# Two transformer blocks on one core: compression products in units of four, zero-padded keys, six held down-projection units, new order offsets

## The chip, the cores and the metric

The kernel runs on one core of a Trainium2 chip. The time is device microseconds (us) of one execution; the number that counts is the median of several runs. Weights and activations lie in HBM at the start and the result is written back to HBM.

## What is computed

The reference applies two layers of a first block and then two layers of a second block to one sequence of 256 tokens of width 1024, all in float32. The part that matters here, cut down:

```python
# first block, per layer (i = 0, 1)
z = rms_norm(h) @ w_in                      # 1024 -> 2328: q, k, v, gates, two MLP halves
kc = compress(zkc, ...); vc = compress(zvc, ...)
def compress(t, pe, w1, b1, w2, b2):        # 15 blocks of 32 tokens per group, 2 groups
    flat = (blocks + pe).reshape(..., 32 * 64)
    return gelu(flat @ w1 + b1) @ w2 + b2   # w1: 2048 x 256
s_s = q @ k_sel.T ; s_w = q @ k_win.T       # 8 heads of 64, 2 key groups, causal mask
attn = gated sum of softmax(s) @ v over the compressed, selected and window keys
h = h + rms_norm(concat(attn, spatial_gating(zu, zv)) @ w_o)
h = h + rms_norm((silu(g) * up) @ w_down)   # g, up: causal convolution over h @ w_up, 1024 -> 2 x 2816
h = h + sigmoid(rms_norm(h) @ w_ple_gate) * (p @ w_ple_proj)
# second block, per layer: another mixer (MLA attention, gated linear attention, pooling),
# then an FFN of the same width without convolution
```

## The kernel before

Every operation is written down by a recorder (class `Recorder`) and put into an order by a list scheduler (`schedule`, line 370), which gives each operation a start from estimated durations, and takes, on each engine, the ready operation of the lowest priority number. The priority is the operation's place in the recording plus an offset from the table `SHIFT`, keyed by phase, group and kind; `HOLD` delays operations and `ALT` moves single operations to another engine (a cast from ScalarE to VectorE, a subtraction from VectorE to GpSimd). The phases are `m1` (first block's mixer), `f1`, `f1m`, `f1e` (its FFN), `p1` (its last gate, called the gate below), `m2` and `f2`... (second block). `emit` (line 523) then issues everything in that order; so all instructions have line 529 in the profile, and are told apart by the tiles they write and read. An operation recorded as `tensor.multi` is several products that stay together.

A weight of 512 KB is loaded into one of 7 buffers `raw`, split into a rounded high part `wh` and a remainder `wl` (5 buffers each; ScalarE casts, VectorE or GpSimd subtracts), and a linear layer is the sum of three products, high by high, high by low and low by high. These products are of type float32r. Others (transposes, attention, compression) are plain float32, which TensorE runs as two passes; the trace shows each pass as a row of its own. PSUM has four pairs of banks: `pa`, `pb`, `upp`, `trp`.

`first_mix` (line 1297) weaves generators: the q projection with `compress_g(0)`, then `qk_g` and `attend_g(0)` with another projection and `compress_g(1)`, then `attend_g(1)` with the rest (lines 1578 to 1583). In `compress_g` (line 1349) four weights of 512 KB are loaded for each of the two inputs (keys, values). Each has four products with 32 stationary columns, which write four strips of 32 partitions of one bank `trp`; the loop records each product separately, so the scheduler may put others between them. There are 2 layers x 2 inputs x 16 = 64 of them. In `attend_g` the scores of a head are one product: queries of 64 partitions (the head's key group `gp`) by both kinds of keys, 256 columns for the first block of queries and 512 for the second, followed by a bf16 product that adds the mask. There are 2 layers x 2 x 8 = 32 score products.

`ffn` (line 1180) goes over 22 units of 128 hidden features: up products into `upp` and `trp`, then the unit's down products into `pa` (first 128 tokens) and `pb` (second). The down products of the last `HELD` units are kept back: first all of the first 128 tokens, then the others, so that the norm after the first half runs beside the products of the second. What follows (the gate, or the next layer's first linear) needs that norm. The held units' weights are split into spare buffers for `HELD - 2` units and into `wh`, `wl` for the last two.

Of the kernel before, what the change touches and what calls it, by code (L numbers as in the profile page):

```python
# [10 lines left out]
F32R = mybir.dt.float32r  # L11
# [13 lines left out]
HELD = 4  # L25
# [497 lines left out]
def emit(nc, order):  # L523
    for op in order:
# [10 lines left out]
        (0, 0): -76, (0, 2): -1938  # L535
    },
# [4 lines left out]
    },  # L541
# [4 lines left out]
    },  # L546
    "f1m": {
        (1, 0): 3412, (1, 2): -723, (2, 0): -26, (2, 1): 256, (2, 2): -722
    },
# [10 lines left out]
    },  # L560
# [4 lines left out]
    },  # L565
    "f2m": {
        (1, 0): -378, (1, 1): -788, (1, 2): 5203, (2, 0): -2486, (2, 1): -3052
    },
# [261 lines left out]
def tile_two_blocks(ctx: ExitStack, tc: tile.TileContext, A: dict, C: dict, out: bass.AP, stop=None):  # L830
    rec = Recorder()
# [1222 lines left out]
```

## Time and profile before

| what | value |
|---|---|
| runs | 1598.17 us median of 3 (1595.35 to 1600.52) |
| profiled execution, its own time | 1594.12 us |
| its span, first to last instruction | 1592.3 us |
[...]
| TensorE (PE) busy | 1563.9 us, 98% |
| VectorE (DVE), ScalarE (ACT), GpSimd (POOL) busy | 75%, 47%, 27% |
| DMA queues, share of 16 engines | 54% |

A row of the timeline gives the start, the length from the first start to the last end, and how many equal instructions were merged. Products overlap in the pipeline: a product's length is longer than the time until the next one starts, so what it costs is the distance between starts.

### The profile page before, as it was taken

What the parts mean: (1) busy time and instruction counts of PE and PEld (TensorE: products, weight loads), DVE (VectorE), ACT (ScalarE), POOL (GpSimd) and SP (SyncE); (2) the same over time, 40 slices, a digit from 0 to 9 for tenths busy, and PEclk for the clock granted to TensorE, in tenths of its full rate; (3) what the DMA queues carried; (4) which work ended last, traced back from release to release, by engine and by line L of the source; (5) the groups of instructions that cost most, each with busy time, mean ns of one, the idle gap of its engine ahead of it and who ended that gap; (6) DMA issues with size and microseconds to landing.
All of it is one profiled execution on the core that took longest, in us unless ns stands there. A gap on an engine that the chain in (4) does not pass through costs nothing.

```text
span 1592.3 us, 22128 instructions
## 1 busy us (share of the span) xinstructions
PE 1563.9 (98%) x8093; PEld 1273.6 (80%) x8093; DVE 1200.0 (75%) x1881; ACT 746.2 (47%) x1391; POOL 428.8 (27%) x379
## 2 busy tenths in 40 slices
PE   7999999999999999999999999999999999999998
PEld 5667888878667888878887888888888788888886
DVE  5668988898668988898576667778876666577786
ACT  4445665655445665655444234433354343353432
POOL 2222011113232011113243223233432332332423
PEclk9999999999999999999999999999999999999999
DMA  6654666645553666645544455656645444556561
GB/s 228 199 170 126 186 188 186 216 142 153 183 165 105 188 185 188 209 148 163 166 147 146 133 185 178 204 174 185 202 153 178 131 151 148 180 178 191 185 190 62
DMA packets 264149, 270.44 MB, mean 170 GB/s; under 512 B 11767, under 2 KB 196713, under 8 KB 264041
## 3 DMA queue, kind: packets, MB, share of 16 engines
q1 hardware_dynamic: 264041, 269.04, 54.3%
q8 instruction: 63, 1.03, 0.3%
q14 instruction: 45, 0.37, 0.1%
HBM read 267.95 MB, written 1.05 MB: 169 GB/s over the span
## 4 chain that ended last, share of the span: by engine, by line
PE 90%; DVE 4%; ACT 2%; POOL 1%; issue 1%; DMA 1%; SPq 0%; DVEq 0%; POOLq 0%; ACTq 0%
PE pa L529 35%; PE upp L529 20%; PE trp L529 18%; PE pb L529 17%; DVE u L529 1%; DVE wl L529 1%; POOL u L529 1%; ACT junk L529 1%; ACT wh L529 1%; ACT u L529 0%; DVE c_h L529 0%; POOL sm L529 0%; ACT x L529 0%; DMA raw<-in_w_in_dram 0%; DMA c_pi<-in_positions_dram 0%
## 5 line engine op out<-in xcount | busy, mean ns | idle before, releaser
L529 DVE TENSOR_TENSOR wl<-raw,wh 128x1024 fp32r<-128x1024 f32 (+2 forms) x408 | 510.1, 1258 | 108.0 <-ACT wh L529 106.3
L529 ACT CAST wh<-raw 128x1024 fp32r<-128x1024 f32 (+2 forms) x342 | 348.8, 1025 | 354.2 <-PE pb L529 107.1
L529 PE MATMUL pa<-wh,x 128*128 128x512 f32 (+1 forms) x1280 | 434.1, 405 | 5.2 <-ACT wh L529 3.3
L529 PEld LDWEIGHTS pa<-wh,x 128*128 128x128 f32 x1280 | 237.1, 189 | 62.9 <-issue 10.9
L529 POOL TENSOR_TENSOR wl<-raw,wh 128x1024 fp32r<-128x1024 f32 (+3 forms) x72 | 174.7, 2428 | 317.7 <-ACT wh L529 171.7
L529 PE MATMUL pa<-wl,x 128*128 128x512 f32 (+1 forms) x640 | 249.2, 402 | 0.0
L529 PE MATMUL upp<-x,wh 128*128 128x512 f32 x640 | 231.7, 397 | 0.0
L529 PE MATMUL trp<-x,wh 128*128 128x512 f32 x640 | 231.0, 397 | 0.0
L529 POOL TENSOR_TENSOR u<-u,u 128x256 f32<-128x256 f32 (+2 forms) x72 | 86.8, 1206 | 411.0 <-DVE u L529 258.0
L529 PE MATMUL upp<-x,wl 128*128 128x256 f32 x640 | 179.7, 281 | 0.0
L529 PE MATMUL trp<-x,wl 128*128 128x256 f32 x640 | 179.3, 280 | 0.0
L529 DVE CAST wh<-raw 128x1024 fp32r<-128x1024 f32 (+1 forms) x138 | 112.9, 819 | 75.8 <-PE pa L529 37.3
L529 PE MATMUL pb<-wh,x 128*128 128x512 f32 (+2 forms) x496 | 161.9, 382 | 2.8 <-ACT x L529 2.8
L529 PEld LDWEIGHTS upp<-x,wh 128*128 128x128 f32 x640 | 120.1, 188 | 26.9
L529 PEld LDWEIGHTS trp<-x,wh 128*128 128x128 f32 x640 | 119.9, 188 | 26.8
L529 PEld LDWEIGHTS pa<-wl,x 128*128 128x128 f32 x640 | 120.4, 189 | 25.8 <-issue 4.3
L529 PEld LDWEIGHTS upp<-x,wl 128*128 128x128 f32 x640 | 120.7, 189 | 4.8 <-DVE wl L529 0.6
L529 PEld LDWEIGHTS trp<-x,wl 128*128 128x128 f32 x640 | 120.8, 189 | 3.4
L529 PEld LDWEIGHTS pb<-wh,x 128*128 128x128 f32 x496 | 92.5, 189 | 19.5 <-ACT x L529 3.3
L529 DVE TENSOR_TENSOR u<-u,u 128x512 f32<-128x512 f32 (+4 forms) x160 | 101.8, 641 | 5.0 <-ACT u L529 3.7
L529 PE MATMUL pb<-wl,x 128*128 128x512 f32 (+2 forms) x248 | 91.7, 380 | 0.0
L529 ACT ACTIVATE u<-pa,sm 128x512 f32<-128x512 f32 (+2 forms) x62 | 41.2, 674 | 87.9 <-PE pa L529 87.1
(221 smaller groups left out, 2384.9 us busy)
## 6 DMA issues: line engine op xcount, KB each, us to landing
raw<-in_w_in_dram SPq DMA_DIRECT2D x112, 512.0 KB, 3.6
raw<-in_w_up_dram SPq DMA_DIRECT2D x88, 512.0 KB, 4.0
raw<-in_w_ffn_gu_dram SPq DMA_DIRECT2D x88, 512.0 KB, 4.3
raw<-in_w_down_dram SPq DMA_DIRECT2D x44, 512.0 KB, 3.5
raw<-in_w_ffn_down_dram SPq DMA_DIRECT2D x44, 512.0 KB, 4.1
raw<-in_w_o_dram SPq DMA_DIRECT2D x32, 512.0 KB, 3.5
raw<-in_cmp_w_dram SPq DMA_DIRECT2D x16, 512.0 KB, 5.1
raw<-in_w_ple_gate_dram SPq DMA_DIRECT2D x16, 512.0 KB, 3.6
```

What stands on the lines that cost most here:

```text
L529: f(*args, **kw)
```

## The change

Four things, and a new order.

In `compress_g` the four products of a loaded weight become one `multi`, so that no other TensorE operation stands between them. In `qk_g` the transposed keys go to two tiles instead of one, one for each key group, with the other group's 64 partitions set to zero (two GpSimd memsets and two VectorE copies of half the partitions in place of one copy, per half of the tokens); the score product then runs over all 128 partitions of the queries, the padded ones adding nothing. `HELD` goes from 4 to 6: the down products of six units are kept back, the last four units' weights are loaded but split only after the loop, and buffers `ah` and `al` go from 5 to 7. Each held unit gets a group of its own in the recording, so that offsets can apply to it. The planner's duration for the second block's attention products is 145 instead of 112 ns for one. The tables `SHIFT`, `HOLD` and `ALT` are all new.

```diff
-HELD = 4
+HELD = 6
...
-    AH = cls("ah", 5, 256, F32R)
-    AL = cls("al", 5, 256, F32R)
+    AH = cls("ah", 7, 256, F32R)
+    AL = cls("al", 7, 256, F32R)
...
-                hv, lv = split(load(wd[:, ft:ft + 1, :]), spare=ft in fts[-HELD:2 - HELD])
-                pend.append((ft, ah, al, hv, lv))
+                raw = load(wd[:, ft:ft + 1, :])
+                if ft in fts[2 - HELD:]:
+                    pend.append((ft, ah, al, raw))
+                else:
+                    pend.append((ft, ah, al) + split(raw, spare=ft in fts[-HELD:2 - HELD]))
...
+        for n, a in enumerate(pend):
+            rec.group += 1
+            if len(a) == 4:
+                pend[n] = a[:3] + split(a[3])
         for t in range(T):
+            for a in pend:
+                rec.group += 1
+                down_mm(*a, ts=[t])
             rec.group += 1
-            for a in pend:
-                down_mm(*a, ts=[t])
...
-        qT, kT = [], unit("kT").rearrange("p (b n) -> p b n", b=2)
+        qT, kT = [], [unit("kT").rearrange("p (b n) -> p b n", b=2) for g in range(2)]
...
-                nc.vector.tensor_copy(kT[:, :, tok(t)], ps[:, 0:2])
+                for g in range(2):
+                    gp, go = slice(g * 64, (g + 1) * 64), slice((1 - g) * 64, (2 - g) * 64)
+                    nc.gpsimd.memset(kT[g][go, :, tok(t)], 0.0)
+                    nc.vector.tensor_copy(kT[g][gp, :, tok(t)], ps[gp, 0:2])
...
-                for r in range(4):
-                    nc.tensor.matmul(ps1[32 * r:32 * r + 32, :256], X[:, 4 * mq + r], raw[:, r], start=(mq == 0),
-                                     stop=(mq == 3))
+                nc.tensor.multi([mm(ps1[32 * r:32 * r + 32, :256], X[:, 4 * mq + r], raw[:, r], start=(mq == 0),
+                                    stop=(mq == 3)) for r in range(4)], 436.0)
...
-                    nc.tensor.matmul(S[:, e], qT[t][gp, j0 + e], kT[gp, :, 0:(t + 1) * 128], start=True, stop=False)
+                    nc.tensor.matmul(S[:, e], qT[t][:, j0 + e], kT[g][:, :, 0:(t + 1) * 128], start=True, stop=False)
...
-                nc.tensor.multi(calls, 2 * 112.0 * len(calls) / 2)
+                nc.tensor.multi(calls, 145.0 * len(calls))
...
 SHIFT = {
     "c1": {
-        (0, 0): -76, (0, 2): -1938
+        (0, 0): 150, (0, 2): -97
     },
```

What the new order does at three places:

TensorE, compression of the first layer's keys (`raw` is a compression weight, `u` the blocks, 32 columns of output partitions each; `upp` belongs to a projection). Before:

```order
L529 MATMUL upp1_223<-wh3_68,x81_76 128x280
L529 MATMUL trp0_224<-raw0_58,u3_82 32x256
L529 MATMUL upp0_222<-wl2_72,x80_75 128x280
L529 MATMUL upp1_223<-wh2_67,x80_75 128x280
L529 MATMUL trp0_224<-raw0_58,u3_82 32x256
L529 MATMUL upp0_222<-wh2_67,x80_75 128x280
L529 MATMUL upp1_223<-wl2_72,x80_75 128x280
L529 MATMUL trp0_224<-raw0_58,u3_82 32x256
L529 MATMUL trp0_224<-raw2_60,u3_82 32x256 x4
L529 MATMUL upp0_222<-wh2_67,x80_75 128x280
L529 MATMUL upp1_223<-wh2_67,x80_75 128x280
L529 MATMUL trp0_224<-raw4_62,u3_82 32x256
```

With the change:

```order
L529 MATMUL upp1_227<-wh3_68,x80_75 128x280
L529 MATMUL trp0_228<-raw0_58,u5_84 32x256 x4
L529 MATMUL trp0_228<-raw1_59,u5_84 32x256 x4
L529 MATMUL upp0_226<-wl2_72,x80_75 128x280
L529 MATMUL trp0_228<-raw5_63,u5_84 32x256 x4
L529 MATMUL trp0_228<-raw6_64,u5_84 32x256 x4
L529 MATMUL upp0_226<-wh3_68,x80_75 128x280
```

Sixteen products that stood singly or in fours and fives among projection products now stand in two runs of eight with one product between them; the other three compressions have two runs of eight each too, so there are 8 such runs in the program.

TensorE, the end of the first FFN (`ah`, `al` by `wh`, `wl` into `pb` are held down products of the second 128 tokens, `c_h` is the residual whose transposes begin the gate, `x` by `wh` the gate's first products). Before:

```order
L529 MATMUL pb0_220<-wl0_70,ah2_108 128x512
L529 MATMUL pb1_221<-wl0_70,ah2_108 128x512
L529 MATMUL pb0_220<-wh0_65,al2_113 128x512
L529 MATMUL pb1_221<-wh0_65,al2_113 128x512
L529 MATMUL trp1_225<-c_ident0_185,c_h0_186 128x128 x4
L529 MATMUL trp0_224<-c_ident0_185,c_h0_186 128x128 x4
L529 MATMUL pb1_221<-wh0_65,x80_75 128x512
L529 MATMUL pa0_218<-wh3_68,x80_75 128x512
L529 MATMUL pa0_218<-wl3_73,x80_75 128x512
L529 MATMUL pa0_218<-wh3_68,x80_75 128x512 x2
L529 MATMUL pa0_218<-wl3_73,x80_75 128x512
```

With the change:

```order
L529 MATMUL pb0_224<-wh3_68,al6_119 128x512
L529 MATMUL pb1_225<-wh3_68,al6_119 128x512
L529 MATMUL pb0_224<-wh0_65,ah1_107 128x512
L529 MATMUL trp0_228<-c_ident0_189,c_h0_190 128x128 x4
L529 MATMUL pb0_224<-wl3_73,ah1_107 128x512
L529 MATMUL pb0_224<-wh0_65,al1_114 128x512
L529 MATMUL pb1_225<-wh0_65,ah1_107 128x512
L529 MATMUL pb1_225<-wl3_73,ah1_107 128x512
L529 MATMUL pb1_225<-wh0_65,al1_114 128x512
L529 MATMUL trp1_229<-c_ident0_189,c_h0_190 128x128 x4
L529 MATMUL pa1_223<-wh2_67,x80_75 128x512
L529 MATMUL pa1_223<-wl0_70,x80_75 128x512
```

Five held products now stand between the transposes of the first and of the second group of features, where the eight transposes stood together.

ScalarE, the start of the program (`raw` is the first weight, `junk` the sums of squares of the input `c_h`, `x` the normalised input). Before:

```order
L529 ACTIVATE junk0_184,sm0_118<-c_h0_186 128x512
L529 COPY c_cols_pre_mix_g0_189<-trp0_224 128x16
L529 ACTIVATE junk0_184,sm0_118<-c_h0_186 128x512
L529 ACTIVATE junk0_184,sm2_120<-c_h0_186 128x512
L529 CAST x80_75<-u4_83 128x4x128
L529 ACTIVATE junk0_184,sm2_120<-c_h0_186 128x512
L529 CAST x80_75<-u6_85 128x4x128
L529 CAST x81_76<-u7_86 128x4x128
L529 CAST wh1_66<-raw1_59 128x1024
L529 CAST wh0_65<-raw0_58 128x1024
```

With the change:

```order
L529 CAST wh0_65<-raw0_58 128x1024
L529 CAST c_ident_b0_195<-c_ident0_189 128x128
L529 ACTIVATE junk0_188,sm0_122<-c_h0_190 128x512
L529 COPY c_cols_pre_mix_g0_193<-trp0_228 128x16
L529 ACTIVATE junk0_188,sm0_122<-c_h0_190 128x512
L529 ACTIVATE junk0_188,sm2_124<-c_h0_190 128x512
L529 CAST x80_75<-u6_85 128x4x128
L529 ACTIVATE junk0_188,sm2_124<-c_h0_190 128x512
L529 CAST x81_76<-u7_86 128x4x128
L529 CAST wh2_67<-raw2_60 128x1024
```

The first weight's cast now stands ahead of everything; its load is the first in SyncE's queue too, ahead of the identity, the gains and the four loads of the input, where it was behind them.

## Rows read from the trace of the kernel before

**Rows 1.** The page's busy times, and the shares of the chain that ended last.
```profile
PE 1563.9 (98%) x8093; PEld 1273.6 (80%) x8093; DVE 1200.0 (75%) x1881; ACT 746.2 (47%) x1391; POOL 428.8 (27%) x379
...
PE 90%; DVE 4%; ACT 2%; POOL 1%; issue 1%; DMA 1%; SPq 0%; DVEq 0%; POOLq 0%; ACTq 0%
```

**Rows 2.** Two stretches: length; busy PE, PEld, DVE, ACT, POOL; clock; DMA share; GB/s.
```profile
40.00:60.00 20.00, 20.00 (x106) 13.31 (x107) 10.73 (x22) 5.42 (x10) 2.37 (x5) 1.00 0.91 293
60.00:80.00 20.00, 20.00 (x80) 10.87 (x78) 16.30 (x32) 11.22 (x45) 6.14 (x9) 1.00 0.32 100
```

**Rows 3.** A wait of PE: us in total, times, longest.
```profile
PE pb L529 <- ACT x L529: 2.8, 2, 1.4
```

**Rows 4.** Timeline of PE, compression products one by one: start, length, operation.
```profile
90.06 0.49 PE L529 MATMUL pa<-wh,x 128*128 128x512 f32 x1
90.49 0.62 PE L529 MATMUL trp<-raw,u 128*32 128x256 f32 x2
91.03 0.49 PE L529 MATMUL pa<-wl,x 128*128 128x512 f32 x1
```

**Rows 5.** Timeline of PE, five compression products (ten passes) in a run.
```profile
43.00 0.28 PE L529 MATMUL upp<-wl,x 128*128 128x280 f32 x1
43.22 1.05 PE L529 MATMUL trp<-raw,u 128*32 128x256 f32 x10
44.20 0.52 PE L529 MATMUL upp<-wh,x 128*128 128x280 f32 x2
44.65 0.62 PE L529 MATMUL trp<-raw,u 128*32 128x256 f32 x2
```

**Rows 6.** Timeline of PE, score products over 64 partitions, 256 columns.
```profile
62.51 0.28 PE L529 MATMUL upp<-c_causal_b,c_ident_b 128*128 128x256 bf16 x1
62.72 0.70 PE L529 MATMUL upp<-u,u 64*128 64x256 f32 x2
63.35 0.28 PE L529 MATMUL upp<-c_causal_b,c_ident_b 128*128 128x256 bf16 x1
```

**Rows 7.** Timeline of PE: a 64-partition product of 512 columns, then one over 128 partitions.
```profile
115.78 1.12 PE L529 MATMUL upp<-u,u 64*128 64x512 f32 x2
116.84 0.28 PE L529 MATMUL upp<-c_causal_b,c_ident_b 128*128 128x256 bf16 x1
116.96 1.02 PE L529 MATMUL pa<-u,u 128*128 128x512 f32 x2
117.82 0.38 PE L529 MATMUL trp<-c_ident,u 128*128 128x128 f32 x2
```

**Rows 8.** Timeline of PE, a float32 product of 256 columns over 128 partitions.
```profile
852.11 0.60 PE L529 MATMUL upp<-u,c_gla_tri 128*128 128x256 f32 x2
852.54 0.59 PE L529 MATMUL upp<-u,c_gla_a 128*128 128x256 f32 x2
```

**Rows 9.** Groups by form: ScalarE's casts, VectorE's subtracts, GpSimd's memsets; busy us, mean ns.
```profile
L529 ACT CAST wh<-raw 128x1024 fp32r<-128x1024 f32 x316 | 330.6, 1051 | 334.2 <-PE pb L529 102.2 <-PE pa L529 82.3 <-PE trp L529 54.9
...
L529 DVE TENSOR_TENSOR wl<-raw,wh 128x1024 fp32r<-128x1024 f32 x384 | 490.9, 1285 | 105.5 <-ACT wh L529 104.0
...
L529 POOL MEMSET u<- 64x256 f32 x14 | 6.2, 447 | 0.5
```

**Rows 10.** Timeline of PE, the end of the first FFN and the start of its gate.
```profile
346.59 0.39 PE L529 MATMUL pa<-wh,al 128*128 128x512 f32 x1
346.82 0.40 PE L529 MATMUL pa<-wh,ah 128*128 128x512 f32 x1
...
352.96 0.50 PE L529 MATMUL pb<-wh,x 128*128 128x512 f32 x1 [1.44 <-ACT x L529]
```

**Rows 11.** Timeline of PE, the first linear product of the program.
```profile
14.22 1.22 PE L529 MATMUL pa<-wh,x 128*128 128x512 f32 x2 [3.33 <-ACT wh L529]
```

**Rows 12.** DMA issues, KB each and median us to landing; the first stretch's DMA share, GB/s.
```profile
raw<-in_cmp_w_dram SPq DMA_DIRECT2D x16, 512.0 KB, 5.1
...
0.00:14.00 14.00, 4.40 (x17) 3.17 (x17) 5.72 (x14) 7.82 (x15) 3.53 (x10) 1.00 0.79 276
```

More of the change, by code (lines that the diff above doesn't have):

```diff
@@ L534 @@
     "c1": {
-        (0, 0): -76, (0, 2): -1938
+        (0, 0): 150, (0, 2): -97
     },
     "f1": {
[3 rows of a table removed]
[3 rows of a table added]
     },
     "f1e": {
[3 rows of a table removed]
[6 rows of a table added]
     },
     "f1m": {
-        (1, 0): 3412, (1, 2): -723, (2, 0): -26, (2, 1): 256, (2, 2): -722
+        (1, 0): 1282, (1, 1): -68, (1, 2): -723, (2, 1): 135, (2, 2): -728
     },
     "f2": {
[9 rows of a table removed]
[9 rows of a table added]
     },
     "f2e": {
[3 rows of a table removed]
-    },
-    "f2m": {
-        (1, 0): -378, (1, 1): -788, (1, 2): 5203, (2, 0): -2486, (2, 1): -3052
[6 rows of a table added]
     },
     "m1": {
[21 rows of a table removed]
[21 rows of a table added]
     },
     "m2": {
[38 rows of a table removed]
[38 rows of a table added]
     },
     "p1": {
[5 rows of a table removed]
[5 rows of a table added]
     },
     "s": {
-        (0, 0): -2115, (0, 2): -1198
+        (0, 0): -391, (0, 2): 1037
     },
     "s2": {
-        (0, 0): -141
+        (0, 0): -161, (0, 2): -2255
     },
@@ L646 @@
 HOLD = {
-    "c1": {
-        (0, 2): 138
-    },
     "f1": {
-        (0, 0): 94, (1, 2): 845, (2, 2): 374, (8, 2): 173, (13, 1): 186
+        (1, 2): 909, (2, 2): 66, (3, 1): 1497, (4, 2): 1406, (6, 2): 818, (12, 2): 171, (14, 0): 824, (14, 1):
+        1184
     },
     "f1e": {
-        (1, 0): 134, (2, 1): 75, (3, 1): 1197, (5, 0): 596, (5, 1): 589, (11, 2): 30, (12, 2): 33, (13, 2): 32
+        (2, 1): 741, (6, 0): 206, (6, 1): 750, (8, 1): 365, (12, 1): 204, (13, 1): 106, (16, 2): 328, (17, 2):
+        36, (19, 2): 566, (22, 2): 335, (23, 2): 102, (25, 2): 394, (28, 2): 37, (29, 2): 260
     },
     "f1m": {
-        (1, 0): 1493, (1, 1): 240, (2, 0): 110, (2, 1): 445
+        (1, 1): 240, (2, 1): 437
     },
     "f2": {
[4 rows of a table removed]
[4 rows of a table added]
     },
     "f2e": {
-        (1, 1): 325, (2, 1): 2288, (4, 1): 1742, (6, 0): 256, (9, 2): 588, (11, 2): 634, (12, 2): 259
-    },
-    "f2m": {
-        (1, 0): 91, (2, 0): 137, (2, 1): 1887
+        (2, 0): 1664, (4, 1): 280, (5, 1): 226, (14, 1): 36, (26, 2): 30, (33, 2): 702, (34, 2): 26
     },
     "m1": {
[7 rows of a table removed]
[7 rows of a table added]
     },
     "m2": {
[14 rows of a table removed]
[15 rows of a table added]
     },
     "p1": {
-        (3, 2): 2, (6, 2): 126, (7, 0): 591, (7, 1): 281, (8, 0): 60, (10, 1): 1394, (12, 1): 384, (13, 0): 909,
-        (20, 2): 169
+        (6, 2): 832, (9, 0): 162, (10, 0): 673, (10, 2): 210, (12, 0): 76, (14, 0): 10, (15, 0): 90, (15, 1):
+        76, (18, 2): 153, (20, 2): 431
     },
     "s": {
-        (0, 2): 600
+        (0, 2): 439
     },
     "s2": {
-        (0, 0): 254, (0, 2): 458
+        (0, 2): 458
     },
@@ L708 @@
     "c1": {
-        7
+        7, 13
     },
     "f1": {
-        3, 25, 28, 61, 75, 79, 82, 121, 140, 196
+        3, 11, 25, 61, 100, 121, 125, 136, 140, 196
     },
     "f1e": {
-        50, 51, 87, 120, 155, 186, 244, 255, 300, 310, 311, 356, 367, 400
+        1, 19, 40, 70, 87, 118, 137, 155, 186, 254, 261, 310, 311
     },
     "f1m": {
-        51, 110, 118
+        51
     },
     "f2": {
-        13, 32, 35, 130, 131, 170, 191, 212, 216, 241, 262, 279, 307, 325, 347, 364, 372, 431, 432, 455, 457,
-        458, 472, 513, 515, 516, 534, 555, 578, 581, 605, 637, 662, 664, 667, 702, 720, 724, 726, 728, 744, 764,
-        765, 786, 787, 823
[3 rows of a table added]
     },
     "f2e": {
-        19, 22, 40, 45, 48, 84, 106, 108, 126, 143, 164, 169, 170, 173, 187, 226, 231, 232, 234, 259, 280, 281,
-        284, 288, 305, 308, 331, 335
-    },
-    "f2m": {
-        2, 22, 40, 45, 48, 63, 81, 85, 106, 108, 110
+        22, 48, 63, 85, 102, 106, 164, 168, 169, 170, 187, 188, 209, 226, 230, 231, 232, 255, 258, 281, 282,
+        286, 303, 329, 372, 376, 377, 378, 381, 402, 420, 425, 433, 476
     },
     "m1": {
[4 rows of a table removed]
[4 rows of a table added]
     },
     "m2": {
[7 rows of a table removed]
[7 rows of a table added]
     },
     "p1": {
-        16, 18, 32, 37, 100, 103, 105, 123, 142
+        16, 18, 37, 39, 100, 142, 169
     },
     "s": {
-        6, 11, 12, 27
+        5, 27
     },
     "s2": {
-        18, 21, 34, 35, 36, 43, 48
+        7, 18, 21, 27, 33, 34, 35, 36, 48
     },
```

246 rows, old and new, of tables (ALT, HOLD, SHIFT) are left out of this document.

## The prediction

> **What bounds the kernel now.** Of the page I read the busy times and the chain first: PE is busy for 1563.9 of the 1592.3 us of the span, and 90% of the chain that ended last is PE [rows 1]. So PE bounds it, and only 1592.3 − 1563.9 = 28.4 us are idle in PE. The granted clock is 1.00 in the stretches that I use [rows 2]; nothing is to be had there. The waits of PE come next: the longest after the start are two of 1.4 us for ScalarE's `x` [rows 3], one at each end of a first-block FFN. Then comes the timeline of PE, start to start, because with a full pipeline a product costs what it holds back the next one; the busy sums hide that. What the reader is to see: a change can gain by shortening what TensorE issues, and by some microseconds at the borders. A few hundred products of the mixers are odd (32 columns, 64 partitions), and these are what the change touches.
>
> **A, compression in runs.** Each of the 64 products has 32 stationary columns and two passes. Alone among full products: from one `pa` product to the next, with a compression product between, 91.03 − 90.06 = 0.97 us [rows 4]; a full 512-column product costs 346.82 − 346.59 = 0.23 [rows 10], so 0.97 − 0.23 = 0.74 is the single's price. In a run of five: from 43.00 to 44.65 lie ten passes and three `upp` products of 280 columns [rows 5]; these are estimated at 0.23 × 280/512 = 0.13 each, so 1.65 − 0.39 = 1.26, say 1.2, for five: the passes of different strips start together. By the issue order of the kernel before, one layer has 15 singles, two runs of five, a four and a three. At 0.74, 1.2, and 0.75 for a four and for a three (a single's length, as no strip gets more than one) this is 11.1 + 2.4 + 1.5 = 15.0, and 30.0 for two layers. After, there are 8 runs of eight in the program. In a run of eight each strip gets two products, as the fullest strip in a run of five does: 1.2 each, 9.6 in all. **30.0 − 9.6 = 20.4 us less.** Bounds: if the second four begins only when the first ends, a run costs 2 × 0.75 = 1.5 and the gain is 18; if eight cost no more than four (0.75 each), it is 24. I take 20.4, as the five is the nearest row.
>
> **B, padded keys.** The 32 score products change from 64 partitions to 128, with equal columns: 16 of 256 and 16 of 512. Over 64 partitions 256 columns take 63.35 − 62.72 = 0.63 [rows 6] and 512 columns 116.84 − 115.78 = 1.06 [rows 7]; over 128 partitions the same widths take 852.54 − 852.11 = 0.43 [rows 8] and 117.82 − 116.96 = 0.86 [rows 7]. Each is 0.20 dearer over 64. The mask product ahead of a 64-partition one costs 62.72 − 62.51 = 0.21 [rows 6], ahead of a full one 116.96 − 116.84 = 0.12 [rows 7]; so entering costs 0.09 more. (0.20 + 0.09) × 32 = **9.3 us less**. Bounds: 6.4 if the entry cost comes from something else; 11 if leaving adds 0.05 that I don't separate.
> The row shows that no two 64-partition products run beside each other here: they start 0.63 and 1.06 apart, more than full ones. [...]
> Padding adds 8 memsets of GpSimd (two keys' groups, two token halves, two layers) at 0.45 us [rows 9], 3.6 us on an engine that is 27% busy [rows 1], and replaces 4 copies of VectorE by 8 of half the partitions; VectorE has 9.3 and 3.7 us of 20 free in the two stretches [rows 2]. I put both at nothing. If the cover is gone, the price is a memset and a copy ahead of the scores, under 1 us in each of 4 places: 4 us.
>
> **C, six held units, borders.** At the end of the first FFN the gate's first product waits 1.44 us for ScalarE's `x` [rows 10], and the second layer's the like: 2.8 us in two waits [rows 3]. Now five held products, 5 × 0.23 = 1.15 us, stand between the two groups of transposes; that work is only moved, so it covers up to 1.15 of each wait: **2 us less**. Bounds: 2.8 if both waits go; the other way, four of the held units are split only after the loop. If the splits come late, PE waits for a cast of 1.05 and a subtract of 1.29 [rows 9]: 2.3 us at each of the four FFNs, 9 us more. I stay near the gain, because other held units' products stand ahead of the late splits as cover: a unit has six products for one token half, 6 × 0.23 = 1.4 us, and the next split is made beside them.
>
> **D, start.** The first linear product starts at 14.22 us, after 3.33 of waiting for ScalarE's cast `wh` [rows 11]. That cast now leads ScalarE's order, and its load SyncE's queue: at best 3.3 less. But the 512 KB stand ahead of the identity, the gains and the input, and this stretch moves 276 GB/s [rows 12]: 512 KB / 276 = 1.9 us later for them, 1.9 more at worst. I take **1 less**; the norm of the input, which needs that input, then ends last.
>
> **The rest.** The other 7,500 or so TensorE products are the same in number and shape; 145 for 112 ns in the planner's book and all the tables only change the order. Zero, by some 3 us either way, since PE's small waits there are a few us altogether.
>
> Sum: −20.4 − 9.3 − 2 − 1 = −32.7. The profiled execution took 1594.1 us; the median 1598.2 stands 4.1 above it. So 1561.4 for a profile, and **1565.5** for the median. Ends of the sum: all gains at their best, 24 + 11 + 2.8 + 3.3 + 3 = 44 less, 1554; all at their worst, 18 + 6.4 − 4 − 9 − 1.9 − 3 = 6.5 less, 1592; they will not all fall together, and the forecast's own range is 1556 to 1574.
>
> **The rivals.**
> 1. *Half the gain.* Once PE needs some 15 us less per mixer of the first block, another engine or the loads end last there. For it: in 40 to 60 us DMA is at 0.91, in 60 to 80 VectorE is busy for 16.3 of 20 us [rows 2]; such stretches can shrink by 9% and 18% only. Against: they are two of many, and the neighbours have room. Then only A stays: 1598.2 − 20.4 = 1578.
> 2. *Slower: the buffers.* A run of eight needs two compression weights in `raw` at once, and the order keeps up to four of the seven buffers with them; such a load takes 5.1 us to land [rows 12]. The projections' weights behind them start late and PE waits ahead of each of the 8 runs. It decides when a run loses over 32.7 / 8 = 4.1 us; at a whole landing, 5.1, it gives 1565.5 + 41 = 1606. For it the DMA share of 0.91; against it that no wait of PE for a load stands among those now, and that the singles also held a buffer until the last of four.
> 3. *A full-array product costs double the 64-partition one.* Then B turns from −9.3 to 16 × (0.63 + 1.06) = +27, and the time is 1565.5 + 9.3 + 27 = 1602. [...]
> 4. *The strips don't overlap in runs* (the change doesn't do what it says): A is nothing, 1565.5 + 20.4 = 1586. The five in 1.2 us speaks against it [rows 5].
> 5. *More.* The order also closes most of the waits at start and borders and small ones elsewhere: of 28.4 idle us some 10 more go, 1555.
>
> **How the numbers follow.** Chances: forecast 0.74, rival 1 0.13, 2 0.03, 3 0.02, 4 0.03, 5 0.05. A measurement of this kernel tells some 0.3%, 4.8 us, from no change. Faster takes the forecast and rivals 1, 4 and 5: 0.95; rival 3, 4 us up, is same: 0.02; rival 2 slower: 0.03. The range leaves out rivals 2 to 4 and the far ends of the rest: 1554 to 1581.
>
> **What would show it.** Right: PE busy falls by some 30 us with PE still above 97%; each run of eight spans about 1.2 us start to start; padded score products stand 0.43 and 0.86 apart; the waits for `x` at the FFN ends are under 0.5; the first linear product stands near 13. Wrong: PE waits for `raw` ahead of the compression, DMA at 0.95 through the mixer (rivals 1, 2), padded products at 1.2 and over (3), runs of eight over 4 us (4), or waits on `wl` at the FFN ends (C's bound).

## The result and the profile after

The changed kernel takes **1550.52 us** (median of 4 runs, 1549.35 to 1551.15) against 1597.12 (median of 4, 1595.35 to 1600.52): ratio 0.9705, interval 0.9687 to 0.9723, so 46.6 us faster. The forecast was 1565.5 with a range from 1554 to 1581: the direction was right, the gain was 1.4 times the forecast's 32.7 us, and the time lies 3.5 us under the range. The profiled execution took 1550.35 us, its span is 1548.4, so between the two profiles it is 43.8 us.

The page after, busy times and the shares of the chain:

```profile
PE 1527.8 (99%) x8093; PEld 1273.8 (82%) x8093; DVE 1187.0 (77%) x1878; ACT 756.9 (49%) x1410; POOL 413.9 (27%) x375
...
PE 96%; DVE 1%; DMA 1%; ACT 1%; issue 0%; SPq 0%; POOL 0%; DVEq 0%; POOLq 0%; ACTq 0%
```

Beside [rows 1], PE is busy 36.1 us less with the same number of passes, and its idle time falls from 28.4 to 20.6 us. It is still PE that bounds the kernel, 96% of the chain against 90%. The granted clock is 0.998 against 0.999: up to the last product it was 1.00 throughout before, and after it was 0.50 in one stretch, from 15.5 to 18.9 us, where TensorE's intervals cost 1.7 us over the usual. So the clock explains none of the gain between the two profiles. PE's waits after (us in total, times, longest):

```profile
PE trp L529 <- DMA u<-in_pre_mix_g_dram: 5.1, 1, 5.1
PE pa L529 <- ACT x L529: 2.6, 3, 2.0
PE trp L529 <- DMA c_h<-in_x_dram: 2.4, 2, 1.8
PE trp L529 <- DVE c_h L529: 1.0, 2, 0.5
```

The two waits of [rows 3] are gone, and so are all waits for `ah` and `wl`. The timeline of PE after, at the places of [rows 4 to 11]:

```profile
11.28 0.78 PE L529 MATMUL pa<-wh,x 128*128 128x512 f32 x1
...
15.16 0.56 PE L529 MATMUL pa<-wh,x 128*128 128x512 f32 x1 [2.04 <-ACT x L529]
...
39.19 1.07 PE L529 MATMUL trp<-raw,u 128*32 128x256 f32 x16
40.20 0.39 PE L529 MATMUL upp<-wl,x 128*128 128x280 f32 x1
40.52 0.42 PE L529 MATMUL trp<-raw,u 128*32 128x256 f32 x4
...
53.14 0.27 PE L529 MATMUL upp<-c_causal_b,c_ident_b 128*128 128x256 bf16 x1
53.25 0.60 PE L529 MATMUL upp<-u,u 128*128 128x256 f32 x2
53.68 0.27 PE L529 MATMUL upp<-c_causal_b,c_ident_b 128*128 128x256 bf16 x1
...
73.91 1.13 PE L529 MATMUL upp<-u,u 128*128 128x512 f32 x2
74.87 0.27 PE L529 MATMUL trp<-c_ident,u 128*128 128x128 f32 x1
...
328.72 0.39 PE L529 MATMUL pb<-wh,ah 128*128 128x512 f32 x1
328.95 0.60 PE L529 MATMUL trp<-c_ident,c_h 128*128 128x128 f32 x4
...
330.32 0.39 PE L529 MATMUL pb<-wh,al 128*128 128x512 f32 x1
331.23 0.66 PE L529 MATMUL trp<-c_ident,c_h 128*128 128x128 f32 x4 [0.52 <-DVE c_h L529]
331.68 0.49 PE L529 MATMUL pa<-wh,x 128*128 128x512 f32 x1
```

Read by distance between starts: a run of eight, 16 passes, takes 40.20 − 39.19 = 1.01 us, and 0.19 more in the projection product between it and the next run (40.52 − 40.20 = 0.32 where 0.13 is usual): the 1.2 of the prediction. A padded score product takes 53.68 − 53.25 = 0.43 at 256 columns, as forecast, and 74.87 − 73.91 = 0.96 at 512, 0.10 more than [rows 7] had for a full product (the 16 of this width take 0.86 to 0.96); the mask ahead of it takes 0.11 (0.21 in [rows 6]). The gate's first product follows its transposes without a wait; what is left at that border is 0.52 us ahead of the second transposes.

**Where 44 us went.** I sorted every interval between neighbouring starts of PE once: those that begin or end at a compression product, at a score or mask product, those that end in a wait shown by the trace, and all others. From each the usual spacing of the same product (median over both traces) is taken off; the compression, score and mask products themselves are counted whole. In us:

| part | before | after | measured | forecast |
|---|---|---|---|---|
| A, at compression products | 28.5 | 9.2 | −19.4 | −20.4 |
| B, at score and mask products | 36.4 | 28.0 | −8.5 | −9.3 |
| C, waits at the ends of the two first-block FFNs | 4.4 | 1.9 | −2.5 | −2 |
| D, first linear product, and waits up to 17 us | 14.7 | 13.5 | −1.2 | −1 |
| other waits | 12.4 | 5.9 | −6.6 | 0 |
| other intervals over the usual spacing | 28.3 | 23.0 | −5.3 | 0 |
| from the last product's start to the end | 7.3 | 6.8 | −0.5 | 0 |

The four priced parts came within 1 us each, 31.6 of 32.7. The 12.4 us in the last three lines lie in what the forecast called the rest. Sorted by place, they lie in the main in the first block, not the second. Waits outside the start and the FFN ends and other intervals over the usual, without the stretch at clock 0.50, sum to 18.9 us before and 9.7 after in the first block (up to 735 us before and 705 after), and to 19.0 and 15.5 in the second (here the usual spacing is that of equal tiles and shapes, and the sums come out somewhat lower than the table's). Of the intervals that end in no wait shown, 116 were over the usual by more than 0.1 us before (16.5 us together), and 72 after (10.1 us).

### The profile page after: what moved, and what is told of

Its sections match the earlier page's. It is cut to its first block, busy times and chain, and to the rows that moved or that the text cites. A ratio compares the mean times of both kernels' runs of the same rounds, so it can differ in the third digit from the quotient of the medians.

```text
span 1548.4 us, 22146 instructions
## 1 busy us (share of the span) xinstructions
PE 1527.8 (99%) x8093; PEld 1273.8 (82%) x8093; DVE 1187.0 (77%) x1878; ACT 756.9 (49%) x1410; POOL 413.9 (27%) x375
## 3 DMA queue, kind: packets, MB, share of 16 engines
HBM read 267.95 MB, written 1.05 MB: 174 GB/s over the span
## 4 chain that ended last, share of the span: by engine, by line
PE 96%; DVE 1%; DMA 1%; ACT 1%; issue 0%; SPq 0%; POOL 0%; DVEq 0%; POOLq 0%; ACTq 0%
PE pa L529 37%; PE upp L529 21%; PE pb L529 19%; PE trp L529 19%; DVE u L529 1%; DMA raw<-in_w_in_dram 1%; DMA row<-in_post_ffn_g_dram 0%; SPq L529 0%; DVE c_h L529 0%; DMA c_pi<-in_positions_dram 0%; ACT junk L529 0%; DVE wl L529 0%; ACT u L529 0%; POOL sm L529 0%; ACT x L529 0%
## 5 line engine op out<-in xcount | busy, mean ns | idle before, releaser
L529 DVE TENSOR_TENSOR wl<-raw,wh 128x1024 fp32r<-128x1024 f32 (+2 forms) x400 | 498.3, 1254 | 74.8 <-ACT wh L529 68.9
L529 ACT CAST wh<-raw 128x1024 fp32r<-128x1024 f32 (+4 forms) x346 | 353.2, 1027 | 345.9 <-PE pb L529 109.8
L529 PE MATMUL pa<-wh,x 128*128 128x512 f32 (+1 forms) x1280 | 426.7, 402 | 4.0 <-ACT x L529 2.6
L529 POOL TENSOR_TENSOR wl<-raw,wh 128x1024 fp32r<-128x1024 f32 (+1 forms) x80 | 191.2, 2391 | 533.2 <-ACT wh L529 388.0
L529 DVE CAST wh<-raw 128x1024 fp32r<-128x1024 f32 (+2 forms) x134 | 97.2, 726 | 55.3 <-PE pa L529 28.0
L529 POOL TENSOR_TENSOR u<-u,u 128x512 f32<-128x512 f32 (+4 forms) x60 | 73.6, 1227 | 240.5 <-DVE u L529 144.4
L529 DVE TENSOR_TENSOR u<-u,u 128x512 f32<-128x512 f32 (+4 forms) x172 | 113.1, 663 | 12.2 <-ACT u L529 9.1
L529 PEld LDWEIGHTS pb<-wh,x 128*128 128x128 f32 x496 | 91.9, 189 | 15.5 <-ACT wh L529 1.0
L529 PE MATMUL trp<-c_ident,u 128*128 128x128 f32 (+4 forms) x399 | 77.8, 274 | 6.4 <-DMA u<-in_pre_mix_g_dram 5.1
```

What stands on the lines that cost most here:

```text
L529: f(*args, **kw)
```

## The experiments

In the first four the planner is run anew, so more may move than the edit says. In the others a step behind the planner moves single instructions of one engine, or gives an operation to another engine at the same place of the order, and keeps everything else as it was; there a move is written (engine, first, end, to): the instructions from first up to end go ahead of instruction to.

**Score products over 64 partitions** (label rows64), the changed kernel with part B undone:

```diff
-nc.tensor.matmul(S[:, e], qT[t][:, j0 + e], kT[g][:, :, 0:(t + 1) * 128], start=True, stop=False)
+nc.tensor.matmul(S[:, e], qT[t][gp, j0 + e], kT[g][gp, :, 0:(t + 1) * 128], start=True, stop=False)
```

> The changed kernel, but its 32 score products run over the key group's own 64 partitions again; memsets, copies and the order of every engine stay as they are. Theory (0.29 us dearer for each, as priced in the prediction): 9 us slower than the changed kernel, about 1559 to 1560 us. Rival (the unexpected 14 us of the change sit in this edit): 15 us or more slower, above 1565. Rival (products over 64 partitions overlap and cost half): faster than the changed kernel.

Measured 1558.55 us (1557.34 to 1559.45), 8.0 above the changed kernel. The order is the changed kernel's on every engine. In its trace one product of 512 columns has this place (timeline of PE):

```profile
96.23 1.12 PE L529 MATMUL upp<-u,u 64*128 64x512 f32 x2
97.28 0.28 PE L529 MATMUL upp<-c_causal_b,c_ident_b 128*128 128x256 bf16 x1
```

97.28 − 96.23 = 1.05, as in [rows 7]; by the sorting above, B is 36.3 again, 8.4 more than after. So B is worth what it was priced at, and halving the contraction paid nothing here: a product of 512 columns takes 1.05 us over 64 partitions, and 0.86 to 0.96 over 128. The rival in which the products over 64 partitions overlap and cost half did not come true: they are the dearer ones. No two of them stand next to each other in this order (a product of another kind follows each), so whether two of them would run side by side was not tested.

**Compression products recorded singly** (singles), the changed kernel with part A undone as far as the planner let it:

```diff
-nc.tensor.multi([mm(ps1[32 * r:32 * r + 32, :256], X[:, 4 * mq + r], raw[:, r], ...) for r in range(4)], 436.0)
+for r in range(4):
+    nc.tensor.matmul(ps1[32 * r:32 * r + 32, :256], X[:, 4 * mq + r], raw[:, r], ...)
+rec.local -= 3
```

(The last line keeps the numbering that `ALT` goes by.)

> The changed kernel with the compression products recorded one by one, so that the scheduler puts others between them: 11 stand singly, one pair, two runs of six, three of five, three of eight. Theory (a single 0.74, a run of five to eight 1.2 us): 8.1 + 0.75 + 6.0 + 3.6 = 18.5 against 9.6 us, 9 us slower, about 1559 us. Rival (the compression gained by the new order and not by the runs): within 3 us of the changed kernel.

Measured 1583.03 us (1582.38 to 1584.55), 32.5 above the changed kernel, not 9. The intervals at compression products are 17.8 us, 8.6 more, as priced. The other 24 come with the order. In the first block's two mixers (17 to 160 us, and 345 to 530 with the first gate) the intervals that end in a wait of PE grow from 2.7 and 1.3 us over the usual to 10.2 and 10.2, and the largest sum is this one (waits of PE):

```profile
PE trp L529 <- ACT u L529: 7.9, 5, 3.4
```

Some 7 us more are lost at a lower clock behind these waits (below, after the four runs). The new tables were made for a recording in which four products are one step; that the same numbers put other things late when it is recorded otherwise is the likely reason, not a shown one.

**Four held units** (held4), the changed kernel with `HELD = 4`:

```diff
-HELD = 6
+HELD = 4
```

> The changed kernel with four held units instead of six; the tables stay. Theory (the two further held units removed the waits at the ends of the FFNs): the 1.4 us waits for x at the borders and the waits for wl come back, 5 to 9 us slower. Rival (the new order removed them): within 3 us of the changed kernel, and PE's waits at the borders stay under 0.7 us each.

Measured 1587.62 us (1584.07 to 1589.70), 37 above, far over both theories. By the sorting, PE's waits from the first linear product on come to 34 us against 10. Two of them:

```profile
PE pa L529 <- ACT ah L529: 4.9, 2, 3.2
...
PE pb L529 <- ACT x L529: 1.8, 1, 1.8
```

The waits that the first theory named are back, 1.8 and 2.2 us for `x` at the two borders (341.5 and 700.0 us) and 2.3 for `wl`. But longer ones stand at the ends of the FFNs, for `ah` above all, which neither theory has: `HELD` also shifts the groups that the tables of this phase are keyed by. How much of the 37 us is missing cover, and how much tables that no longer fit, this run can't tell.

**The old tables** (oldtab), the changed kernel with `SHIFT`, `HOLD` and `ALT` of the kernel before.

> The changed kernel with the order tables of the kernel before; all other edits stay. Theory (the 14 us that the prediction lacked come from the new order): 10 to 20 us slower than the changed kernel, with PE's waits and small delays back to those of before and the compression and score products as cheap as after. Rival (they come from the held units): within 4 us of the changed kernel.

Measured 1635.13 us (1631.20 to 1636.04): ratio 1.0227 to the kernel before, interval 1.0207 to 1.0247. The edits of the code without their order are slower than the kernel before by 2%. The compression and score products stay cheap (10.2 and 29.3 us), and the waits of PE take it all back:

```profile
PE pa L529 <- ACT ah L529: 20.4, 6, 6.2
```

This is far over the expected 10 to 20 us, and over the 12.4 us that it was to explain. So the run shows that this code needs tables made for it; whether an order made as well for the old code would have had the 12.4 us, it can't tell.

**What the lower clock adds.** In the last three runs not all of the loss is waiting. The rows at the first gate of run before_runs (next) show it best, since the kernel before has the same wait of 1.44 us there [rows 10] and has a clock of 1.00 behind it (timeline of PE, then the stretch with its clock, in the columns of [rows 2]):

```profile
343.74 0.52 PE L529 MATMUL pb<-wh,x 128*128 128x512 f32 x1 [1.44 <-ACT x L529]
344.07 0.62 PE L529 MATMUL pa<-wh,x 128*128 128x512 f32 x1
344.49 0.63 PE L529 MATMUL pa<-wl,x 128*128 128x512 f32 x1
...
344.10:347.50 3.40, 3.40 (x10) 2.58 (x9) 2.95 (x6) 0.83 (x3) 2.20 (x2) 0.50 0.24 83
```

At 0.50 a product of 512 columns takes 344.49 − 344.07 = 0.42 us where 0.23 is usual. Summed over all such stretches ahead of the last product (us in the profiled execution; both sums over the usual spacing):

| run | span over the changed kernel's | intervals that end in a wait, from 17 us on | other intervals at clock 0.50 | length of these stretches |
|---|---|---|---|---|
| changed kernel | | 6.4 | 1.7 | 3.4 |
| singles | 32.7 | 22.1 | 9.1 | 20.5 |
| held4 | 39.5 | 30.4 | 12.7 | 27.3 |
| oldtab | 85.8 | 59.7 | 24.3 | 58.0 |

In these three runs the stretches begin within or shortly behind waits of PE, of 0.9 to 6.2 us in all but one of them (in held4 at 450.5 us, where the wait ahead is 0.3). So some of the price of a long wait is paid after it, at the lower clock: 7 to 23 us in these runs, beside 16 to 53 us of the waits themselves.

**Part A alone in the kernel before** (before_runs), only TensorE's compression products moved, 7 of each eight:

```diff
     order = schedule(rec, classes)
+    order = rearrange(order, classes, [('tensor', 128, 129, 140), ('tensor', 130, 131, 140), ...])
```

> The kernel before, its order kept on every engine, with only the 64 compression products moved on TensorE: of each eight that belong to two loaded weights the first seven are issued just ahead of the eighth. Theory (part A as priced): PE's intervals at these products fall from 28.5 to some 9 us, 20 us faster than the kernel before, about 1577 us. Rival (the weights' buffers, held some microseconds longer, stop the loads): new waits of PE for casts or loads eat half or more of it, above 1586.

Measured 1577.66 us (1576.61 to 1578.65) against 1596.18: ratio 0.9880, interval 0.9867 to 0.9894, 18.5 us faster. The intervals at these products fall from 28.5 to 8.8 us. The rival's waits are small: 0.7 us for `wl` at two places, which were not there before. Part A stands alone and adds to the rest. In the profiled execution the granted clock was 0.50 in three stretches (from 13.0, 105.1 and 344.1 us), so the comparison is that of the medians, whose runs have like clocks (0.995 to 0.999 before, 0.996 and 0.997 in this run).

**The FFN's products on VectorE** (before_dve). The trace of the kernel before shows in the first FFN, on PE and what it waits for:

```profile
231.24 1.79 POOL L529 TENSOR_TENSOR u<-u,u 128x256 f32<-128x256 f32 x1 [3.32 <-ACT u L529]
...
232.86 0.28 PE L529 MATMUL trp<-x,wl 128*128 128x256 f32 x1
...
233.07 0.41 ACT L529 CAST ah<-u 128x256 fp32r<-128x256 f32 x1 [0.96 <-POOL u L529]
...
233.53 0.49 PE L529 MATMUL pa<-wh,ah 128*128 128x512 f32 x1 [0.39 <-ACT ah L529]
233.86 0.39 PE L529 MATMUL pa<-wl,ah 128*128 128x512 f32 x1
234.09 0.40 PE L529 MATMUL pa<-wh,ah 128*128 128x512 f32 x1
```

The last product of the gated unit runs on GpSimd and takes 1.79 us; the cast that waits for it lets the down products start late. The idle time is 0.39, but the interval 233.53 − 232.86 = 0.67 stands where 0.12 is usual, and the next, 0.33, where 0.23 is: 0.65 us in all. The edit:

```diff
+    for op in order:
+        if op.eng == "gpsimd" and op.key[0] in ("f1", "f1m", "f1e") and op.meth == "tensor_tensor" \
+                and op.kw["op"] == ALU.mult and list(op.args[0].shape[1:]) == [256]:
+            op.eng = "vector"
```

> The kernel before, its order kept, with the 20 products of 128x256 that GpSimd does in the first block's FFNs done by VectorE at the same place of the order. Theory (the waits for ah in the FFNs come from GpSimd's 1.8 us): four waits of 0.65 and three of 0.3 us are gone, 3 to 4 us faster, about 1594 us. Rival (VectorE's 8 us more make the subtracts late): PE waits for wl instead, no gain or slower.

Measured 1593.30 us (11 runs, 1591.05 to 1595.87) against 1596.18: ratio 0.9978, interval 0.9969 to 0.9987, 2.9 us faster. The group of these products, before, in this run, and in the changed kernel (busy and mean, then idle time ahead of them):

```profile
L529 PE MATMUL pa<-wh,ah 128*128 128x512 f32 x160 | 63.7, 404 | 1.8 <-ACT ah L529 1.5
```
```profile
L529 PE MATMUL pa<-wh,ah 128*128 128x512 f32 x160 | 63.1, 400 | 0.0
```
```profile
L529 PE MATMUL pa<-wh,ah 128*128 128x512 f32 x160 | 63.0, 396 | 0.0
```

The new `ALT` table makes the same move: from 160 to 345 us GpSimd does 17 such multiplications before and 5 after (operations on tile `u`, with the shortest, middle and longest time in ns):

```profile
L529 POOL TENSOR_TENSOR u<-u,u x17: 737/1292/2197, 193.7 to 337.7; 128x256 f32<-128x256 f32 x10, 128x512 f32<-128x512 f32 x7
```
```profile
L529 POOL TENSOR_TENSOR u<-u,u x5: 735/742/1592, 160.1 to 313.5; 128x256 f32<-128x256 f32 x5
```

So this is one piece of the missing gain, some 3 us, and it has nothing to do with the four edits in the code. A wait of 0.70 us for `wl` at 313.5 us is new; run before_runs has one like it, so it need not come from VectorE's added work. The profiled execution, 1595.71 us, was one of the slowest of the eleven: in the mixer, where nothing was edited, it has a wait of 1.86 us at 130.0 where the kernel before had 0.78, and behind it a clock of 0.50 from 132.2 to 139.0 us.

**The cover at the border** (cover), the changed kernel with six held products moved ahead, at both first-block FFN ends:

```diff
     order = schedule(rec, classes)
+    order = rearrange(order, classes, [('tensor', 1588, 1594, 1579), ('tensor', 3301, 3307, 3292)])
```

> The changed kernel, its order kept, with six held products for the second tokens moved at the ends of both first-block FFNs from behind the last product for the first tokens to ahead of the last eight of them. Theory (the products behind that last product cover the norm of the first tokens, and the six held units pay by leaving 18 of them where there were 10): the first transposes of the residual wait 1.2 to 1.4 us at each of the two places, 2.5 us slower than the changed kernel. Rival (the norm is early anyway): under 0.5 us.

Measured 1552.44 us (1551.58 to 1553.51), 1.9 above the changed kernel (timeline of PE):

```profile
328.69 0.39 PE L529 MATMUL pb<-wh,ah 128*128 128x512 f32 x1
330.16 0.66 PE L529 MATMUL trp<-c_ident,c_h 128*128 128x128 f32 x4 [1.09 <-DVE c_h L529]
```

The first transposes, which did not wait after, wait 1.09 us; by the sorting, 1.25 us more at each of the two places. So what shortens the border is the number of held products behind the last one for the first 128 tokens: 18 after, 12 here, 10 before. Of these, 13, 7 and 10 stand ahead of the first transposes; the five between the transposes are in both new orders, and what they are worth by themselves was not tested.

**Two single moves** (plus), the changed kernel with one cast on ScalarE and one product on VectorE moved ahead:

```diff
     order = schedule(rec, classes)
+    order = rearrange(order, classes, [('scalar', 10, 11, 9), ('vector', 159, 160, 157)])
```

In the changed kernel both stand behind something that waits for a load (all engines' timeline):

```profile
13.55 1.04 ACT L529 CAST wh<-raw 128x1024 fp32r<-128x1024 f32 x1 [2.68 <-DMA raw<-in_w_in_dram]
14.50 0.61 ACT L529 CAST x<-u 128x512 fp32r<-128x512 f32 x1
...
116.33 0.17 DVE L529 CAST c_pf<-c_pi 128x2 f32<-128x2 int32 x1 [1.59 <-DMA c_pi<-in_positions_dram]
...
117.00 0.68 DVE L529 TENSOR_TENSOR x<-u,x 128x512 fp32r<-128x512 f32 x1
117.74 0.50 PE L529 MATMUL pa<-wh,x 128*128 128x512 f32 x1 [0.68 <-DVE x L529]
```

> The changed kernel with two single moves: on ScalarE at the start a cast of x goes ahead of a cast of wh that waits for its load, and on VectorE near 116 us a product for x goes ahead of a cast that waits 1.6 us for the positions' load. Theory: the two waits of PE that stand behind them (2.0 us at 15.2 and 0.7 us at 117.7) shrink by 0.3 to 1.4 and by 0.9 us, 1.2 to 2.3 us faster than the changed kernel. Rival (the loads of the weights come next at the start, another operand at 117): under 0.7 us in all.

Measured 1548.44 us (1547.95 to 1548.97). The wait at 117.7 us is gone. At the start 2.04 us become 0.61, but the next load then ends last (timeline of PE), and the stretch at clock 0.50 from 15.5 us on, which cost the changed kernel 1.7 us, is not there:

```profile
13.66 0.74 PE L529 MATMUL pa<-wh,x 128*128 128x512 f32 x2 [0.61 <-ACT x L529]
...
15.55 0.73 PE L529 MATMUL pb<-wh,x 128*128 128x512 f32 x2 [0.93 <-ACT wh L529]
```

The same two kernels once more on one chip, first the changed one:

> The changed kernel itself, beside the version with two moves on the same chip: about 1550.5 us.

> The version of run plus once more, on the same chip as the changed kernel. Theory (the two moved instructions were worth 2 us): 1.5 to 2.5 us under the changed kernel, the two ranges apart. Rival (the difference between the two runs was the chip's): ranges that overlap.

1549.06 us (1547.73 to 1550.46) and 1547.95 (1547.44 to 1548.13). The spans of the two profiles differ by 2.4 us (1548.5 and 1546.1), the medians by 1.1, and the ranges overlap: better by one to two us, not clear of the spread. As before, the changed kernel's profile has a stretch at clock 0.50 at the start (from 15.8 us) and the other has none, so part of the difference is the clock's. It has the lowest median measured.

**Two more moves at the border** (plus2), run plus with the residual's second update and the product behind the transposes ahead of a subtract of 1.2 us:

```diff
+  ('vector', 502, 503, 500), ('vector', 501, 502, 500), ('vector', 1002, 1003, 1000), ('vector', 1001, 1002, 1000)
```

> The kernel of run plus with two more moves on VectorE at the ends of both first-block FFNs: the second update of the residual, and the product behind the first transposes, go ahead of a subtract of 1.2 us for the gate's weights. Theory (PE's 0.5 us wait there, 0.7 us with its refill, comes from that subtract): both waits gone, 1.4 us faster than run plus, about 1547 us. Rival (the subtract, now later, makes PE wait for wl in the gate): under 0.5 us, or slower.

Measured 1548.73 us (1548.05 to 1549.79): no gain. The wait ahead of the second transposes is gone, and the product behind them waits as long (timeline of PE):

```profile
328.69 0.60 PE L529 MATMUL trp<-c_ident,c_h 128*128 128x128 f32 x4
329.83 0.50 PE L529 MATMUL pa<-wh,x 128*128 128x512 f32 x1 [0.53 <-ACT x L529]
```

What ends last there is now ScalarE's `x`, not `wl` as the rival had it: taking one wait away uncovered the next, of the same length.

**The gate's additions on VectorE** (before_gate), one profile. In the kernel before, at the end of the second gate (all engines):

```profile
732.44 1.30 POOL L529 TENSOR_TENSOR c_h<-c_h,u 128x512 f32<-128x512 f32 x1 [1.35 <-DVE u L529]
732.45 1.84 DVE L529 TENSOR_TENSOR x<-u,x 128x512 fp32r<-128x512 f32 x1
...
734.35 0.45 PE L529 MATMUL pa<-wh,x 128*128 128x400 f32 x1 [0.63 <-DVE x L529]
```

```diff
+    for op in order:
+        if op.eng == "gpsimd" and op.key[0] == "p1" and op.meth == "tensor_tensor" and op.kw["op"] == ALU.add \
+                and list(op.args[0].shape[1:]) == [512]:
+            op.eng = "vector"
```

> The kernel before, its order kept, with the six additions to the residual that GpSimd does in the two gates done by VectorE. Theory (the subtract for x took 1.84 us for two at 732.4, the first of them slow because GpSimd worked beside it): the two subtracts take 1.4 us, and PE's wait of 0.63 us at 734.3 shrinks to 0.2 or less although VectorE has 0.7 us more to do. Rival (VectorE is simply late): the wait grows to 1 us or more.

The row is one subtract, not two as I wrote. In this run (all engines):

```profile
732.06 0.69 DVE L529 TENSOR_TENSOR x<-u,x 128x512 fp32r<-128x512 f32 x1
732.67 0.68 DVE L529 TENSOR_TENSOR c_h<-c_h,u 128x512 f32<-128x512 f32 x1
733.15 0.53 PE L529 MATMUL pa<-wh,x 128*128 128x400 f32 x2
```

0.69 us where it took 1.84, and PE's wait, 0.80 us by its interval, is gone altogether. VectorE was not late; by these rows its subtract took 1.15 us longer beside GpSimd's addition of 1.30 us, by what mechanism no run shows. The time, 1593.09 us, is that of a single run and lies 1.3 us below the fastest of the kernel before beside it; it decides nothing. The changed kernel has no wait at this place either, but by another way: the additions are still GpSimd's, and the subtract starts first (701.37 us, 0.69 long; the addition at 701.54 then takes 1.67).

## Why the prediction was wrong, step by step

**Right:** A (19.4 of 20.4, and 18.5 alone in the kernel before), B (8.5 of 9.3, and 8.0 when it is undone), D (1.2 of 1). In A the bound at which a run of eight costs two runs of four did not come: at 39.19 us the run takes 1.01, and the passes of the four strips start 6 to 8 ns apart. In B only the full product of 512 columns was dearer than [rows 7], 0.96 for 0.86. C had the right size, 2.5 for 2, but not the place: I let the five products between the transposes cover the wait as work that is only moved, while run cover shows that it goes by how many held products stand behind the last one for the first tokens, 18 for 10; so its size was partly luck. In D the first linear product came 2.94 us earlier, at 11.28, near the best that I allowed, and a wait of 2.04 behind it took more than half of that back.

**The step that failed is "The rest", "Zero, by some 3 us either way, since PE's small waits there are a few us altogether."** It measured −12.4: 6.6 in waits, 5.3 in intervals that the trace shows no wait for, 0.5 at the end. Three things were wrong with it. First, the waits outside the start and the FFN ends were not a few us: the idle column alone has 15 of them with 7.4 us before (after: 10 with 3.3). Second, a wait costs more than its idle time: the row at 233.53 shows 0.65 us lost for 0.39 idle, and by the distance between starts these waits came to 12.4 us. Third, I gave the new tables no direction, and had no term for intervals that are long without a wait. I had named more as rival 5, with 0.05 and 10 idle us; but PE's idle time fell by only 7.8 us in all, C and D included, and the rest of the gain stood in what the page counts as busy.

Runs oldtab, held4 and singles bear on this only in part. Away from the recording that the tables were made for, this code loses 85, 37 and 24 us, in waits and at the lower clock behind them. That shows how much an order can cost here, not that the new order brought the 12.4 us; that it did is an inference, since the other edits were priced and measured, and runs before_dve and before_gate show single pieces.

**The second piece** is the base. I carried the profiled execution's distance to the median, 4.1 us, over to the changed kernel. The kernel before spreads over 1594.4 to 1600.5 in all the runs here, and its profile, 1594.12, was faster than all of them; the changed one spreads over 1547.7 to 1551.2, and its profile took 1550.35 with a median of 1550.52. That is 3.9 us of the 15.0 that the forecast missed; the rest gives 12.4, and A, B, C and D together take 1.1 back (rounding makes up the difference). The distance goes with the granted clock: of the 40 runs of the kernel before beside the experiments, the ten at 0.999, the profile's clock, took 1594.4 to 1595.8 us, the 16 at 0.996 or less 1595.8 to 1600.4. So part of what the change brings in the median, and not between the profiles, may be stretches at the lower clock that no longer follow its waits; the unprofiled runs don't show where theirs were.

**Rivals.** Nothing waits for compression weights (rival 2); the mixers are still PE's (rival 1); rival 3 fell with run rows64, as no run shows its doubled price (512 columns take 0.86 to 0.96 us over 128 partitions, and 1.05 over 64); rival 4 with before_runs.

**What stays open:** of the 12.4 us some 3 are shown to be GpSimd's multiplications in the first block's FFNs, and 0.8 one place in a gate, a wait that the changed kernel has no longer. For the other 8 or 9, most of them in the first block, no single edit was found and the cause is open; and how much of it needs six held units cannot be told from a run with four, since the tables may not fit there.

## What to carry to other kernels

Price a wait by the distance between starts, not by its idle time, and the next product with it (0.65 us for 0.39 idle at 233.53); and look at the granted clock behind it, since a wait can be followed by a stretch at half the clock (0.50 from 344.1 to 347.5 us in run before_runs, behind a wait of 1.44). A kernel at 98% of one engine can still hold ten microseconds of small waits (12.4 in the table above, before), which here went along with a retuned order; so a change that comes with a new order needs a term for it, with a range, taken from the sum of all waits. And ask of each wait what stands ahead on the releasing engine: twice it was an instruction waiting for a load, twice a GpSimd operation, and once, when the one was moved, the next in the chain was as late.

## What the runs showed of the hardware

- Products of four different 32-column strips start almost together: in the single records of the changed kernel's run of eight at 39.19 us, four passes start 6 to 8 ns apart and the next four 0.20 to 0.22 us behind the last of them, so these eight products of 256 columns cost 1.0 us, 1.2 with the way in; alone one costs 0.74 [rows 4].
- A float32 product over 64 partitions takes 1.05 us for 512 columns and 0.63 for 256, 0.1 to 0.2 more than over 128 partitions (0.86 to 0.96, and 0.43), and the mask product ahead of it 0.1 more (0.21 against 0.11).
- A multiplication of 128x256 on GpSimd takes 0.74 us at best and 1.79 in the row above; a VectorE subtract of 128x512 takes 0.69 alone (run before_gate) and 1.84 in the kernel before, where it begins 0.01 us behind a GpSimd addition of 1.30 us. The 1.84 is near the sum of both, 0.69 + 1.30 = 1.99: the subtract ends at 734.29, 0.55 behind the addition's end at 733.74. By what mechanism it is held up no run shows.
- A wait of 0.39 us of idle time cost 0.65 (the kernel before, 233.53): the first product behind it starts some 0.16 later than the idle time alone explains, and the second 0.10 later than usual.
- The granted clock fell from 1.00 to 0.50 for a few microseconds within or behind some waits of TensorE (3.4 us from 15.5 in the changed kernel, 6.8 from 132.2 in run before_dve), and not behind others: behind the same wait of 1.44 us for `x` at the end of the first FFN it stayed at 1.00 in the trace of the kernel before and was 0.50 in that of before_runs, from 344.1 to 347.5 us. A product of 512 columns there starts 0.42 us behind the last instead of 0.23.
